# A third gate/up pair by quarter products, and a new order of casts, lesser parts and gates in two FFN openings

## The chip, the core and the metric

The kernel runs on one core of a Trainium2 chip. TensorE (PE) multiplies, VectorE (DVE) and ScalarE (ACT) do the elementwise work, GpSimd (POOL) issues some DMAs, and SyncE (SP) issues most of the others. Each engine works through its own queue in order; semaphores tie the queues together. The metric is the time of one execution in microseconds.

## The reference

The reference is one residual block over 512 tokens of width 1024:

```
h = h + 0.5 * swiglu_1(rmsnorm(h))                 # D_FF = 2816
z = rmsnorm(h) @ W_in ; conv module and gated linear attention
h = h + concat([y_conv, y_gla]) @ W_out
h = h + 0.5 * swiglu_2(rmsnorm(h))
h = h + sigmoid(rmsnorm(h) @ W_g) * (p @ W_p)
out = rmsnorm(h)
swiglu(x) = (silu(x @ W_gate) * (x @ W_up)) @ W_out
```

All of it is float32. The kernel holds every operand of a product as a high part (H, `wh`: the value rounded to the product's format) and a lesser part (L, `wl`: what is left of it), and does three products for each: high by high, high by lesser, lesser by high.

## The kernel before

**Pairs.** Each FFN layer takes the 2816 columns of gate and up in 11 pairs: a pair is 256 gate columns with the 256 up columns that belong to them. Its four weight tiles are `a11`, `a12` (gate, upper and lower half of the 1024 rows) and `a21`, `a22` (up). Each is fetched by one 512 KB DMA on SP into a ring of six buffers (`wr`), cast to `wh` on ACT, and its lesser part `wl` is a subtraction on DVE (`low`). `added` is another way to a lesser part: ACT writes the negated rounded value into `wl`, and a DMA on POOL's queue adds the unrounded `wr` to it.

**Two forms.** A plain pair is eight units h0 to h7, each of 12 products of 512 columns. A quarter pair works on sums and differences of the quarters of the weights and of the activations, as in Strassen's method in Winograd's form, and needs seven units of 24 products of 256 columns instead of what would be eight: m1, m2, m6, m7, m5, m4, m3. Its weights are a11, a12, s2, s3, s1, a22, s4, where s1 = a21 + a22, s2 = s1 - a11 and so on (DVE, tiles `sm` and `wr`); its activations are parts of the normalised input (`hg`) and four sums t1 to t4 of its quarters (DVE differences in tiles `xg`, then a cast `t2H` on ACT and a lesser part `t2L` on DVE, and likewise for the others). m1, m6, m5 and m3 add to one PSUM bank, and what the bank holds in between is needed too: ACT copies it out after m1 (`sq`), after m6 (`u`) and after m5 (`sq` again), and the next unit on that bank waits for the copy. After m2 the gate's first half is ready: two DVE operations and a silu on ACT (`gate0`, tiles `g` and `s`). After m5, m4 and m3 come the up products (`u`), the second half of the gate, the products `m`, and `act_parts`: two casts (`actH`) on ACT and two lesser parts (`actL`) on DVE for the output products.

**Order.** `drive` walks a list of units. Every unit has jobs with a distance: fetch, sum, cast and lesser part of a weight are put into the queues so many units ahead (`AHEAD` = 4 for a lesser part, 5 for m5's). What a unit leaves over (gates, act parts) is put in around the next unit. Output pieces of 24 products of 512 columns (`second`) follow a group of pairs and are strewn among the later units. Hooks at named units put other work in, such as the sums of the activations.

**The two layers.** In the first layer pair 0 is done while the input arrives, pairs 1 and 2 are plain (`plain` = (1, 2)), and pairs 3 to 10 are done by quarters; the sums t1 to t4 are spread over the units of pairs 1 to 3. In the second layer pair 0 is plain and done ahead of `ffn`; pairs 1 to 10 go by quarters. In that layer the first pair's `gate0` is held back to the end of its m5.

Of the kernel before, what the change touches and what calls it, by code (L numbers as in the profile page):

```python
# [62 lines left out]
def block_kernel(ctx: ExitStack, tc: tile.TileContext, a: dict, out: bass.AP):  # L63
    nc = tc.nc
    pe, dve, act, pool = (Ordered(tc, e) for e in (nc.tensor, nc.vector, nc.scalar, nc.gpsimd))
# [117 lines left out]
    def high(r3):  # L183

        nk, nc_ = r3.shape[1], r3.shape[2]
        hi = wp.tile([P, 1024], F32R, tag="wh", bufs=6, name=nm("wh"))
        lo = wp.tile([P, 1024], F32R, tag="wl", bufs=6, name=nm("wl"))
        h3 = hi[:, :nk * nc_].rearrange("p (k c) -> p k c", k=nk)
        l3 = lo[:, :nk * nc_].rearrange("p (k c) -> p k c", k=nk)
        act.copy(h3, r3)  # L190
        return h3, l3, r3

    def low(w, engine=dve):
        h3, l3, r3 = w
        engine.tensor_tensor(out=l3, in0=r3, in1=h3.bitcast(F32), op=ALU.subtract)
        return h3, l3
# [191 lines left out]
    class Left:  # L388


        def __init__(self, w, f):
            self.w, self.f, self.done = w, f, {}

        def fetch(self, *names):
            for name in names:
# [10 lines left out]
        def part(self, name, engine=None):  # L406

            if name not in self.done:
                self.done[name] = low(high(getattr(self, name)), engine or dve)
            return self.done[name]  # L410

        def add_part(self, *names):

# [23 lines left out]
    ffn1_in = a["ffn1_w_in"][0]  # L437
# [89 lines left out]
    mid = []  # L527
# [73 lines left out]
        for f in left:  # L601
            f()

    def ffn(w_in, w_out, x, gname, given, first, rsb, hooks, plain):


        norm = Norm()
# [1 line left out]
        got = {}  # L609
        npair = DFF // (2 * P)  # L610
        start = 1 + len(plain)
        held = []
        end = npair - 1
        pairs = {i: given.get(i) or Left(w_in, 2 * i) for i in range(npair)}

# [19 lines left out]
        def scaled(ps, name):  # L635
            o = tmp(name)
            dve.tensor_tensor(out=o, in0=ps, in1=got['rsb'], op=ALU.mult)
            return o

        def gated_block(p, s, u, i):  # L640
            if not hasattr(p, "m"):
                p.m = tmp("m", 2 * SEQ, bufs=1).rearrange("p (f c) -> p f c", f=2)
            dve.tensor_tensor(out=p.m[:, i], in0=u, in1=s, op=ALU.mult)
# [21 lines left out]
        def m2(p):  # L665
            p.y = bank()
            mul(p.y, p.part("a12"), x.op["b21"], True, True)

            def gate0():
                p.s0 = silu(plus(p.y, p.a, 0, "g1"))  # L670

            if p is pairs[start] and not plain:
                held.append(gate0)
                return []
            return [gate0]

# [8 lines left out]
        def m5(p):  # L685
            mul(p.x, p.part("s1"), x.op["t1"], False, False)
            p.u = plus(p.w, snap(p.x, "sq", bufs=3), 1, "u1")
            for f in held:
                f()
            held.clear()  # L690

        def m4(p):
            mul(p.w, p.part("a22"), x.op["t4"], False, True)
# [2 lines left out]
        def m3(p):  # L696
            mul(p.x, p.part("s4"), x.op["b22"], False, True)
            s = silu(times_row(p.x, 1, "g1"))
            return [lambda: gated(p, s, p.u, 1), lambda: act_parts(p)]

        def plain_unit(j):

            up, i, k = j // 4, j // 2 % 2, j % 2
            def run(p):
                if not j:
                    p.g, p.s = {}, {}
                if not k:
                    p.x = bank()
                ps = p.x
                wh, wl = p.part(f"a{1 + up}{1 + k}")  # L710
                cs = slice(i * P, (i + 1) * P)
                for c in range(4):
                    mm3(ps, wh[:, c, cs], wl[:, c, cs], *x.rows[4 * k + c], k == c == 0, k == 1 and c == 3)
                if not k:
                    return []
                if not up:
                    def gate():
                        p.s[i] = silu(scaled(ps, "g1"))
                    return [gate]
                return [lambda: gated_block(p, p.s[i], scaled(ps, "u1"), i),  # L720
                        lambda: act_parts(p) if i else None]
            return run

        USES = {"m1": ("a11", m1), "m2": ("a12", m2), "m6": ("s2", m6), "m7": ("s3", m7), "m5": ("s1", m5),
# [2 lines left out]
        def unit(kind, i):  # L727
            p = pairs[i]

            def go(run):  # L730
                left = run(p)
                hooks.get((kind, i), lambda *_: None)()
                return left

            if kind[0] == "h":
                j = int(kind[1])
                part, run = (f"a{1 + j // 4}{1 + j % 2}", plain_unit(j)) if j % 4 < 2 else (None, plain_unit(j))
                if part:
                    return [(AHEAD, lambda: p.part(part)), (9, lambda: p.fetch(part))], lambda: go(run)
            else:  # L740
                part, run = USES[kind]
            before = [(AHEAD + (kind == 'm5'), lambda: p.part(part))] if part else []
            if kind in ("m1", "m2"):
                before.append((7, lambda: p.fetch(part)))
            elif kind == "m6":
                before += [(9, lambda: p.fetch("a21", "a22")), (6, p.s12)]
            elif kind in ("m7", "m3"):
                before.append((6, p.s3_ if kind == "m7" else p.s4_))

            return before, lambda: go(run)  # L750

        def second(cut):
# [117 lines left out]
    def sums_hooks(x, names, at):  # L870

        h = {}
        for name, key in zip(names, at):
            h[key] = lambda *_, name=name: x.split(name)
        return h

    hooks = sums_hooks(xb, ("t2", "t3", "t1", "t4"), (("h5", 1), ("h7", 1), ("h3", 2), ("m1", 3)))
    hooks.update({("h%d" % (i + 1), 1): f for i, f in enumerate(steps[2:])})
    hooks.update({("m5", 3): lambda *_: made[0](), ("m5", 4): lambda *_: constants(),
                  ("m4", 10): lambda *_: w_ahead.append(ahead(w_in, D_CONV, 2 * P)),  # L880
                  ("last", 4): lambda *_: w_ahead.append(ahead(w_in, 0, 2 * P))})
    hg, norm = ffn(ffn1_in, a["ffn1_w_out"][0], xb, "mix_norm", {0: Left(ffn1_in, 0), 1: w1},
                   (ps0[:2], ps0[2:]), lambda: spread(mid[0]), hooks, (1, 2))
    pool.on = False
    cw, gwu, mean, mask, nbias = made

# [633 lines left out]
    def todo(*fs):  # L1520
# [5 lines left out]
                  ("rest", 2): todo((q_high, b21, q21, 0), (first_sum, 0), (third_sum, 0)),  # L1526
                  ("rest", 4): todo((q_high, b21, q21, 1), (first_sum, 1), (third_sum, 1)),
                  ("rest", 6): todo((final_in,), (row_sums, 0))})
    hg, norm = ffn(ffn2_in, a["ffn2_w_out"][0], xb, "ple_norm", wf, ((g0, u0), (g1_, u1_)), mid[1], hooks, ())

# [269 lines left out]
```

## Time and profile before

| | us |
|---|---|
| median of three runs | 949.35 (947.44 to 949.62) |
| the profiled execution | 948.38 |
| its span, first to last instruction | 946.7 |
| PE, DVE, ACT, POOL busy | 935.0, 755.6, 477.0, 57.2 |
| granted TensorE clock, mean | 0.996 |

A row of a timeline has start, duration, engine, line, operation, output and inputs, size and count; in square brackets stands how long the engine was idle before it and who ended that. All instructions go through one recording helper, line 46, so tiles tell them apart, not lines. Products are pipelined, so the duration of one is longer than the step from one to the next. A row of a window has its limits, the busy time with the number of instructions, the granted clock, the DMA share and GB/s. A row of PE's waits has what waited, for whom, the total, the number of times and the longest.

### The profile page before, as it was taken

To read this page: it belongs to the slowest core of one execution; us is meant where nothing else is said; L and a number is where in the kernel's file an instruction comes from. 1 tells how busy PE (TensorE), PEld (TensorE's weight loads), DVE (VectorE), ACT (ScalarE), POOL (GpSimd) and SP (SyncE) were. 2 spreads that over 40 slices of the span, in tenths; PEclk is the share of its full clock that TensorE was granted. 3 is DMA by queue.
4 is the path that set the end of the run, shared out by engine and by line. 5 is a ranking of instruction groups with operands and counts; after the bars stand their busy time and mean duration, and the time that the engine had idled before them with its cause. 6 is when DMAs were issued, how large, how long until landed. Compare 5 with 4: busy or idle time off the path is not lost.

```text
span 946.7 us, 14553 instructions
## 1 busy us (share of the span) xinstructions
PE 935.0 (99%) x5842; PEld 831.1 (88%) x5842; DVE 755.6 (80%) x1030; ACT 477.0 (50%) x720; POOL 57.2 (6%) x72
## 2 busy tenths in 40 slices
PE   9999999999999999999999999999999999999996
PEld 7888999999999988788877889899999999998885
DVE  5876887887788566999986788887878787866896
ACT  5652544434433574463564874444434433445882
POOL 0000200000000110001030020000000000000121
PEclk9999999999999999999999999999999999999998
DMA  7532323342323593346552572332243224347463
GB/s 229 180 114 72 106 69 117 105 131 80 103 90 111 140 257 83 81 102 167 134 126 77 154 163 82 112 114 88 90 134 112 67 91 133 96 147 225 89 113 110
DMA packets 107831, 113.43 MB, mean 120 GB/s; under 512 B 5155, under 2 KB 96469, under 8 KB 107764
## 3 DMA queue, kind: packets, MB, share of 16 engines
q1 hardware_dynamic: 101732, 94.67, 32.3%
q0 software_dynamic: 6016, 17.83, 10.4%
q8 instruction: 46, 0.75, 0.3%
q14 instruction: 21, 0.17, 0.1%
q10 hardware_dynamic: 16, 0.00, 0.0%
HBM read 93.61 MB, written 2.10 MB: 101 GB/s over the span
## 4 chain that ended last, share of the span: by engine, by line
PE 96%; DVE 2%; ACT 1%; issue 1%; POOLq 0%; POOL 0%; DVEq 0%; ACTq 0%
PE ps L46 94%; PE ax L46 2%; DVE wl L46 1%; DVE g L46 0%; ACT wh L46 0%; DVE u L46 0%; DVE wr L46 0%; ACT s L46 0%; DVE y L46 0%; DVE sm L46 0%; DVE actL L46 0%; DVE hgL L46 0%; ACT wl L46 0%; POOLq L1798 0%; ACT ycH L46 0%
## 5 line engine op out<-in xcount | busy, mean ns | idle before, releaser
L46 PE MATMUL ps<-hgH,wh 128*128 128x256 f32 (+1 forms) x768 | 235.9, 312 | 0.0
L46 PE MATMUL ps<-hgL,wh 128*128 128x256 f32 (+1 forms) x768 | 234.2, 310 | 0.0
L46 PE MATMUL ps<-hgH,wl 128*128 128x256 f32 (+1 forms) x768 | 234.0, 310 | 0.0
L46 DVE TENSOR_TENSOR wl<-wr,wh 128x1024 fp32r<-128x1024 f32 (+2 forms) x162 | 189.6, 1181 | 48.1 <-ACT wh L46 48.0
L46 ACT CAST wh<-wr 128x1024 fp32r<-128x1024 f32 (+2 forms) x177 | 177.8, 1019 | 39.8 <-PE ps L46 19.8
L46 PEld LDWEIGHTS ps<-hgH,wh 128*128 128x128 f32 x768 | 146.9, 192 | 9.9 <-issue 1.1
L46 PEld LDWEIGHTS ps<-hgH,wl 128*128 128x128 f32 x768 | 146.7, 191 | 7.8
L46 PEld LDWEIGHTS ps<-hgL,wh 128*128 128x128 f32 x768 | 146.3, 191 | 8.0 <-issue 0.2
L46 PE MATMUL ps<-actH,wh 128*128 128x512 f32 x352 | 137.4, 390 | 0.0
L46 PE MATMUL ps<-actL,wh 128*128 128x512 f32 x352 | 137.3, 390 | 0.0
L46 PE MATMUL ps<-actH,wl 128*128 128x512 f32 x352 | 136.9, 389 | 0.0
L46 ACT ACTIVATE s<-g 128x512 f32<-128x512 f32 x48 | 30.4, 633 | 190.2 <-DVE g L46 190.2
L46 DVE SCALAR_TENSOR_TENSOR cv<-glu,cw,cv 128x502 f32<-128x502 f32 (+24 forms) x120 | 81.0, 731 | 0.6
L46 PEld LDWEIGHTS ps<-actH,wl 128*128 128x128 f32 x352 | 66.1, 188 | 14.0
L46 PEld LDWEIGHTS ps<-actH,wh 128*128 128x128 f32 x352 | 66.2, 188 | 13.0
L46 PEld LDWEIGHTS ps<-actL,wh 128*128 128x128 f32 x352 | 66.2, 188 | 12.4
L46 DVE SCALAR_TENSOR_TENSOR h<-ps,h 128x512 f32<-128x512 f32 x80 | 53.9, 686 | 21.3 <-PE ps L46 21.2
L46 ACT COPY sq<-ps 128x512 f32<-128x512 f32 x40 | 23.3, 585 | 68.4 <-PE ps L46 68.3
L46 DVE TENSOR_TENSOR wl<-sm,wh 128x1024 fp32r<-128x1024 f32 x40 | 48.7, 1221 | 5.1 <-ACT wh L46 4.9
L46 ACT CAST wh<-sm 128x1024 fp32r<-128x1024 f32 x40 | 41.7, 1043 | 7.0 <-DVE sm L46 4.2
L46 ACT CAST actH<-m 128x512 fp32r<-128x512 f32 x44 | 25.4, 618 | 38.5 <-DVE m L46 38.4
L46 PE MATMUL ps<-t1H,wh 128*128 128x256 f32 x144 | 40.9, 284 | 1.0 <-ACT u L46 1.0
(267 smaller groups left out, 1744.2 us busy)
## 6 DMA issues: line engine op xcount, KB each, us to landing
wr<-in_ffn_w_in SPq DMA_DIRECT2D x84, 512.0 KB
wr<-in_ffn_w_out SPq DMA_DIRECT2D x32, 512.0 KB
wr<-in_w_in SPq DMA_DIRECT2D x20, 512.0 KB
wl<-wr POOLq DMA_DIRECT2D x16, 512.0 KB, 5.5
wr<-in_ffn_w_out SPq DMA_DIRECT2D x16, 384.0 KB
wr<-in_w_out SPq DMA_DIRECT2D x8, 512.0 KB
wq<-in_ple_w_gate SPq DMA_DIRECT2D x8, 512.0 KB
wl<-wq POOLq DMA_DIRECT2D x8, 512.0 KB, 5.3
```

The source lines that it names most:

```text
L46: inst = call(*args, **kwargs)
```

## The change

In the first layer only pair 1 stays plain; pair 2 goes by quarters, so the sums t2, t3 and t1 are made during pair 1 and t4 at pair 2's m1. Some weights get their cast one unit ahead of the lesser part (`cast`, the table CASTS), some lesser parts stand three units ahead instead of four or five (FAR), and two of them, pair 1's a21 and pair 2's a12, are made by `added` (ADDS). In the second layer four distances change, s2 of pair 2 is cast early, and s1 and s3 of pair 2 are cast ahead of pair 1's `gate0`. In both layers `act_parts` of every pair but the last is put behind the next pair's m6 instead of around the unit after m3, and pair 1's last gate product and act parts in the first layer go behind m6 of pair 2.

```diff
+        def cast(self, *names):
+            for name in names:
+                self.cut[name] = high(getattr(self, name))
...
-    def ffn(w_in, w_out, x, gname, given, first, rsb, hooks, plain):
+    def ffn(w_in, w_out, x, gname, given, first, rsb, hooks, plain, far={}, casts={}, adds=()):
...
-            if p is pairs[start] and not plain:
-                held.append(gate0)
+            if p is pairs[start]:
+                after["m5", start] = [gate0] if plain else [lambda: pairs[start + 1].cast("s1", "s3"), gate0]
                 return []
...
-            return [lambda: gated(p, s, p.u, 1), lambda: act_parts(p)]
+            if p is pairs[end]:
+                return [lambda: gated(p, s, p.u, 1), lambda: act_parts(p)]
+            after["m6", p.f // 2 + 1] = [lambda: act_parts(p)]
+            return [lambda: gated(p, s, p.u, 1)]
...
-                return [lambda: gated_block(p, p.s[i], scaled(ps, "u1"), i),
+                last = [lambda: gated_block(p, p.s[i], scaled(ps, "u1"), i),
                         lambda: act_parts(p) if i else None]
+                if i and p is pairs[start - 1]:
+                    after["m6", start] = last
+                    return []
+                return last
...
                 left = run(p)
+                for f in after.pop((kind, i), ()):
+                    f()
                 hooks.get((kind, i), lambda *_: None)()
...
-            before = [(AHEAD + (kind == 'm5'), lambda: p.part(part))] if part else []
...
+            if (kind, i) in casts:
+                before.append((casts[kind, i], lambda: p.cast(part)))
+            if part:
+                make = p.add_part if (kind, i) in adds else p.part
+                before.append((far.get((kind, i), AHEAD + (kind == "m5")), lambda: make(part)))
...
-    hooks = sums_hooks(xb, ("t2", "t3", "t1", "t4"), (("h5", 1), ("h7", 1), ("h3", 2), ("m1", 3)))
-    hooks.update({("h%d" % (i + 1), 1): f for i, f in enumerate(steps[2:])})
+    hooks = sums_hooks(xb, ("t2", "t3", "t1", "t4"), (("h4", 1), ("h5", 1), ("h7", 1), ("m1", 2)))
+    w2 = Left(ffn1_in, 4)
+    hooks.update({("h0", 1): steps[2], ("h1", 1): steps[3],
+                  ("h4", 1): lambda *_: [steps[4](), xb.split("t2")],
+                  ("h5", 1): lambda *_: [xb.split("t3"), w2.s12()]})
...
-                   (ps0[:2], ps0[2:]), lambda: spread(mid[0]), hooks, (1, 2))
+    FAR = {("h5", 1): 3, ("m1", 2): 3}
+    CASTS = {("h5", 1): 4, ("m1", 2): 4}
+    ADDS = {("h4", 1), ("m2", 2)}
...
+                   (ps0[:2], ps0[2:]), lambda: spread(mid[0]), hooks, (1,), FAR, CASTS, ADDS)
...
-    hg, norm = ffn(ffn2_in, a["ffn2_w_out"][0], xb, "ple_norm", wf, ((g0, u0), (g1_, u1_)), mid[1], hooks, ())
+    hg, norm = ffn(ffn2_in, a["ffn2_w_out"][0], xb, "ple_norm", wf, ((g0, u0), (g1_, u1_)), mid[1], hooks, (), {("m5", 1): 4, ("m6", 2): 3, ("m1", 3): 3, ("m2", 3): 3}, {("m6", 2): 4})
```

The first place that the prediction speaks of is DVE's queue in the first layer, behind the act parts of pair 0 (tiles end in a buffer number). Before, from a22's lesser part of pair 1 to that of pair 2's a12:

```order
L46 TENSOR_TENSOR wl_483<-wr_429,wh_482 128x1024
L46 TENSOR_TENSOR xg_416<-xg_422,xg_416 128x512
L46 TENSOR_TENSOR xg_422<-xg_422,xg_413 128x512
L46 TENSOR_TENSOR xg_419<-xg_419,xg_422 128x512
L46 TENSOR_TENSOR g_111_507<-ps_439,bc_457 128x512
L46 TENSOR_TENSOR xg_498<-xg_501,xg_498 128x512
L46 TENSOR_TENSOR xg_501<-xg_527,xg_501 128x512
L46 TENSOR_TENSOR xg_527<-xg_527,xg_498 128x512
L46 TENSOR_TENSOR xg_524<-xg_524,xg_527 128x512
L46 TENSOR_TENSOR wl_549<-wr_431,wh_548 128x1024
L46 TENSOR_TENSOR g_119_552<-ps_511,bc_457 128x512
L46 TENSOR_TENSOR wl_572<-wr_433,wh_571 128x1024
```

Now, behind three differences (`xg`), from the fourth to the lesser part of pair 2's a11, which m1 of pair 2 uses:

```order
L46 TENSOR_TENSOR xg_479<-xg_482,xg_479 128x512
L46 TENSOR_TENSOR wl_491<-wr_429,wh_490 128x1024
L46 TENSOR_TENSOR g_115_519<-ps_436,bc_454 128x512
L46 TENSOR_TENSOR g_121_553<-ps_523,bc_454 128x512
L46 TENSOR_TENSOR xg_482<-xg_508,xg_482 128x512
L46 TENSOR_TENSOR xg_508<-xg_508,xg_479 128x512
L46 TENSOR_TENSOR xg_505<-xg_505,xg_508 128x512
L46 TENSOR_TENSOR t2L_574<-xg_422,t2H_573 128x512
L46 TENSOR_TENSOR t2L_578<-xg_508,t2H_577 128x512
L46 TENSOR_TENSOR sm_581<-wr_512,wr_514 128x1024
L46 TENSOR_TENSOR sm_582<-sm_581,wr_488 128x1024
L46 TENSOR_TENSOR wl_551<-wr_488,wh_550 128x1024
```

The lesser part of a22 (`wr_429`) stands behind four differences now, and t2's lesser parts and pair 2's sums s1 and s2 (`sm`) stand ahead of the first lesser part of pair 2.

The second place is ACT's queue in the second layer at the copy `sq` after pair 1's m1. Before:

```order
L46 ACTIVATE s_5496<-g_960_5494 128x512
L46 CAST wh_5505<-sm_5376 128x1024
L46 COPY sq_5534<-ps_5509 128x512
L46 CAST actH_5536<-m_5492 128x512
L46 CAST actH_5540<-m_5492 128x512
```

Now:

```order
L46 ACTIVATE s_5596<-g_970_5594 128x512
L46 COPY sq_5630<-ps_5605 128x512
L46 CAST actH_5632<-m_5592 128x512
L46 CAST actH_5636<-m_5592 128x512
L46 CAST wh_5640<-sm_5476 128x1024
```

The cast of s1 (`wh<-sm`) has moved from ahead of the copy to behind the act casts of pair 0.

The third place is ACT's queue a little later, from the copy `sq` after pair 1's m5 to the copy `u` after pair 2's m6. Before:

```order
L46 COPY sq_5695<-ps_5509 128x512
L46 ACTIVATE s_5703<-g_987_5700 128x512
L46 CAST wh_5707<-sm_5605 128x1024
L46 CAST wh_5711<-wr_5501 128x1024
L46 ACTIVATE s_5745<-g_996_5742 128x512
L46 CAST wh_5776<-wr_5665 128x1024
L46 ACTIVATE s_5806<-g_1002_5804 128x512
L46 CAST wh_5812<-wr_5705 128x1024
L46 COPY u_1008_5841<-ps_5578 128x512
```

Now:

```order
L46 COPY sq_5794<-ps_5605 128x512
L46 CAST wh_5799<-sm_5705 128x1024
L46 CAST wh_5802<-wr_5601 128x1024
L46 ACTIVATE s_5808<-g_1001_5805 128x512
L46 ACTIVATE s_5845<-g_1006_5842 128x512
L46 ACTIVATE s_5902<-g_1010_5900 128x512
L46 CAST wh_5908<-wr_5765 128x1024
L46 COPY u_1016_5937<-ps_5678 128x512
```

The casts of s1 and s3 of pair 2 stand ahead of pair 1's silu, the cast of pair 3's a11 (`wr_5765`) stands behind the last silu, and that of pair 3's a12 has left the stretch.

More of the change, by code (lines that the diff above doesn't have):

```diff
@@ L391, in __init__ @@
         def __init__(self, w, f):
-            self.w, self.f, self.done = w, f, {}
+            self.w, self.f, self.done, self.cut = w, f, {}, {}
         def fetch(self, *names):
@@ L408, in part @@
             if name not in self.done:
-                self.done[name] = low(high(getattr(self, name)), engine or dve)
+                self.done[name] = low(self.cut.pop(name, None) or high(getattr(self, name)), engine or dve)
             return self.done[name]
+        def cast(self, *names):
+            for name in names:
+                self.cut[name] = high(getattr(self, name))
         def add_part(self, *names):
@@ L611, in ffn @@
         start = 1 + len(plain)
-        held = []
+        after = {}
         end = npair - 1
@@ L687, in m5 @@
             p.u = plus(p.w, snap(p.x, "sq", bufs=3), 1, "u1")
-            for f in held:
-                f()
-            held.clear()
         def m4(p):
@@ L737, in unit @@
                 part, run = (f"a{1 + j // 4}{1 + j % 2}", plain_unit(j)) if j % 4 < 2 else (None, plain_unit(j))
-                if part:
-                    return [(AHEAD, lambda: p.part(part)), (9, lambda: p.fetch(part))], lambda: go(run)
+                before = [(9, lambda: p.fetch(part))] if part else []
             else:
                 part, run = USES[kind]
-            before = [(AHEAD + (kind == 'm5'), lambda: p.part(part))] if part else []
+                before = []
             if kind in ("m1", "m2"):
@@ L881, in block_kernel @@
                   ("last", 4): lambda *_: w_ahead.append(ahead(w_in, 0, 2 * P))})
-    hg, norm = ffn(ffn1_in, a["ffn1_w_out"][0], xb, "mix_norm", {0: Left(ffn1_in, 0), 1: w1},
-                   (ps0[:2], ps0[2:]), lambda: spread(mid[0]), hooks, (1, 2))
+    FAR = {("h5", 1): 3, ("m1", 2): 3}
+    CASTS = {("h5", 1): 4, ("m1", 2): 4}
+    ADDS = {("h4", 1), ("m2", 2)}
+    hg, norm = ffn(ffn1_in, a["ffn1_w_out"][0], xb, "mix_norm", {0: Left(ffn1_in, 0), 1: w1, 2: w2},
+                   (ps0[:2], ps0[2:]), lambda: spread(mid[0]), hooks, (1,), FAR, CASTS, ADDS)
     pool.on = False
```

## The prediction

> **What bounds the kernel now.** I read the page first, then TensorE's waits, then windows over single kinds of products, and last the timelines of the two openings, where an FFN layer starts on its quarter products.
>
> ```profile
> span 946.7 us, 14553 instructions
> PE 935.0 (99%) x5842; PEld 831.1 (88%) x5842; DVE 755.6 (80%) x1030; ACT 477.0 (50%) x720; POOL 57.2 (6%) x72
> ...
> PE ps L46 <- ACT u L46: 1.0, 1, 1.0
> ...
> PE ps L46 <- ACT sq L46: 0.2, 1, 0.2
> ```
>
> TensorE (PE) is busy 99% of the span, so time can be won in two ways only: fewer or shorter products, or fewer waits of PE. Two of its waits name ScalarE (ACT) tiles that this change touches, and both lie in the second layer's opening. How long a product takes is read from start to start:
>
> ```profile
> 38.20:59.96 21.76, 21.76 (x98) 1.00 0.29 91
> 62.76:68.20 5.44, 5.44 (x26) 1.00 0.36 104
> 601.83:607.30 5.47, 5.47 (x27) 1.00 0.32 95
> 621.40:632.90 11.50, 11.50 (x98) 1.00 0.30 93
> ...
> 35.45 0.48 PE L46 MATMUL ps<-hgH,wh 128*128 128x512 f32 x1
> ```
>
> Each window runs from the first start of its products to the start of the next one; the counts take in neighbours that overlap the edges. The first holds eight plain units, 96 products of 512 columns: 21.76/96 = 0.2267 us. The last holds four quarter units, 96 products of 256 columns: 11.50/96 = 0.120 us. So 512 columns cost 0.2267, not 2 x 0.120 = 0.240. The two in the middle are output pieces of 24 products: 5.44 us among products of their own width, 5.47 among quarter units.
>
> **Fewer products (first layer).** Pair 2 leaves the plain form, 96 x 0.2267 = 21.76 us, for seven quarter units, 168 x 0.120 = 20.16 us: **-1.60 us**. Four output pieces now stand among quarter units: 4 x 0.03 = **+0.11 us**, rounded down from 0.12. Everything on PE after them comes earlier, so this is on the path, provided that the operands are ready. The Trainium skill ("TensorE: Matmul & The Clock Gate", Back-to-back issue gap) gives a warm gap of N/2.4 ns plus 2.5 ns, 215.8 and 109.2 ns here; the sum would be 20.72 - 18.34 = 2.38 us saved instead of 1.60. The rows above are some 11 ns longer for either width, and the trace decides.
>
> **The cover in that opening.** The rows on VectorE (DVE) and ACT that price it:
>
> ```profile
> 33.99 1.05 ACT L46 CAST wh<-wr 128x1024 fp32r<-128x1024 f32 x1
> 35.73 0.59 ACT L46 COPY bc<-ax 128x512 f32<-128x512 f32 x1 [0.69 <-PE ax L46]
> ...
> 546.08 1.06 ACT L46 ACTIVATE wl<-wr 128x1024 fp32r<-128x1024 f32 x1
> 547.04 1.03 ACT L46 CAST wh<-wr 128x1024 fp32r<-128x1024 f32 x1
> ...
> 42.62 1.23 DVE L46 TENSOR_TENSOR wl<-wr,wh 128x1024 fp32r<-128x1024 f32 x1 [0.26 <-ACT wh L46]
> 43.76 2.14 DVE L46 TENSOR_TENSOR xg<-xg,xg 128x512 f32<-128x512 f32 x3
> 45.82 0.68 DVE L46 TENSOR_TENSOR g<-ps,bc 128x512 f32<-128x512 f32 x1
> 46.42 0.68 DVE L46 TENSOR_TENSOR xg<-xg,xg 128x512 f32<-128x512 f32 x1
> ...
> 88.05 1.22 DVE L46 TENSOR_TENSOR sm<-wr,wr 128x1024 f32<-128x1024 f32 x1
> 89.30 1.23 DVE L46 TENSOR_TENSOR sm<-sm,wr 128x1024 f32<-128x1024 f32 x1
> ...
> 53.15 0.63 ACT L46 ACTIVATE s<-g 128x512 f32<-128x512 f32 x1 [3.07 <-DVE g L46]
> 53.68 1.03 ACT L46 CAST wh<-wr 128x1024 fp32r<-128x1024 f32 x1
> 54.62 1.14 ACT L46 CAST t2H<-xg 128x512 fp32r<-128x512 f32 x2
> ...
> 553.77 1.05 ACT L46 ACTIVATE wl<-wr 128x1024 fp32r<-128x1024 f32 x1
> ...
> 555.12 0.86 POOL L46 DMA_DIRECT2D wl<-wr  x1 [4.92 <-ACT wl L46]
> ...
> L46 POOL DMA_DIRECT2D wl<-wr x16: 859/862/919, 376.4 to 565.2; - x16
> ...
> DMA to landing us min/median/max: 4.5/5.5/9.9
> ```
>
> From start to start a lesser part (wl) takes DVE 1.14, three chained differences 2.06, a lone 512-wide operation 0.60, two chained sums 1.25 + 1.14.
>
> PE runs h1 from 35.45; with 12 x 0.2267 = 2.72 per plain unit and 2.88 per quarter unit, h4 starts at 43.6, h5 at 46.3, m1 of pair 2 at 54.5, m2 at 57.4. A lesser part is first used in a unit's third product, whose weights load one product earlier: one product after the unit's start.
>
> Pair 1's a21 now gets its lesser part by a negated copy on ACT (0.96, from 546.08 to 547.04) and an accumulating DMA from POOL. The copy follows the cast of 33.99 and pushes bc from 35.73 to 35.89; the gates behind it go 0.16 later, and DVE, which is free at 42.36 in this trace (42.62 less the 0.26 of waiting), is free at 42.5. Then, by the new order: three differences to 44.56, a fourth to 45.16, a22's lesser part done 1.22 later at 46.38, used by h5 at 46.56. Two gate products to 47.5, three differences to 49.56, t2's lesser parts (the first waits for its cast until 49.65) to 50.85, s1 and s2 to 53.24, a11's lesser part of pair 2 done at 54.46, used by m1 at 54.6. Both are in time by 0.1 to 0.2 us, which is less than I can be sure of.
>
> Pair 2's a12 goes the way of POOL: ACT's silu at 46.99 (behind its gate product), cast 47.52, silu 48.46, t2's casts 48.99 and 49.51, a12's cast 50.03, negation 50.97 to 52.03, DMA issued at about 52.3 (0.3 behind, as 555.12 is behind 553.77 + 1.05). With the quickest landing, 4.5, it is there at 56.8, with the median of 5.5 at 57.8; m2 uses it at 57.5. So PE waits 0 to 0.3 us there. I take 0.15 us for all three places, between 0 and 1 us (my timeline may be off by so much). Queued behind: the refill of a21's buffer on SP waits for the first DMA's landing near 41, and the rest of SP's queue with it; it brings pair 3's a11, which ACT casts near 53. Later deadlines have room: s3 is done near 64 for m7 at 66.0, s4 and the up product before m4 (77) for 80.1.
>
> **The second layer's two waits.**
>
> ```profile
> 568.38 0.28 PE L46 MATMUL ps<-hgH,wl 128*128 128x256 f32 x1
> 568.86 0.39 PE L46 MATMUL ps<-t2H,wh 128*128 128x256 f32 x1 [0.20 <-ACT sq L46]
> ...
> 591.87 0.28 PE L46 MATMUL ps<-t3H,wl 128*128 128x256 f32 x1
> 593.10 0.39 PE L46 MATMUL ps<-t1H,wh 128*128 128x256 f32 x1 [0.95 <-ACT u L46]
> ...
> 567.29 1.04 ACT L46 CAST wh<-sm 128x1024 fp32r<-128x1024 f32 x1
> 568.23 0.58 ACT L46 COPY sq<-ps 128x512 f32<-128x512 f32 x1
> ...
> 591.00 0.63 ACT L46 ACTIVATE s<-g 128x512 f32<-128x512 f32 x1 [2.28 <-DVE g L46]
> 591.53 1.03 ACT L46 CAST wh<-wr 128x1024 fp32r<-128x1024 f32 x1
> 592.47 0.58 ACT L46 COPY u<-ps 128x512 f32<-128x512 f32 x1
> ...
> 578.99 0.68 DVE L46 TENSOR_TENSOR u<-ps,sq 128x512 f32<-128x512 f32 x1
> 583.42 1.23 DVE L46 TENSOR_TENSOR wl<-sm,wh 128x1024 fp32r<-128x1024 f32 x1 [1.70 <-ACT wh L46]
> 590.22 0.68 DVE L46 TENSOR_TENSOR g<-ps,bc 128x512 f32<-128x512 f32 x1
> ```
>
> PE's normal step is 0.12, so the first gap, 568.38 to 568.86, holds 0.36 of waiting: m6 cannot add to the bank before ACT's copy sq is out, and that copy stands behind s1's cast. The new order puts the cast behind the copy and the act casts; sq is done at 567.29 + 0.58 = 567.87, before 568.50: **-0.36 us**. s1 is then cast by about 569.9 and its lesser part is done by 571.2; m5 needs it at 574.3, so the cover is three us.
>
> The second gap, 591.87 to 593.10, holds 1.11: m5 of pair 2 needs ACT's copy u out of the bank, and ACT was late because it waits 2.28 for the gate product g of 590.22, a row of DVE. DVE itself had idled 1.70 at 583.42 for a cast. In the new order s1 and s3 of pair 2 are cast before pair 1's silu, so that idle goes; a11's lesser part of pair 3 moves behind g, and s2's comes ahead of it in exchange (1.14 each). The chain from the row u<-ps,sq to g takes 590.22 - 578.99 = 11.23 now. It starts at 578.3 instead (PE is 0.36 earlier, and s2's lesser part no longer stands ahead of it), so g starts at 578.3 + 11.23 - 1.70 = 587.8. Silu, cast and copy follow: the silu from 588.4, the cast from about 589.0, the copy from 589.9 to 590.5. m5 would start at 591.6, so **-1.11 us** goes whole. Late next is a12's lesser part of pair 3: DVE does a11's part behind its cast from 590.05 (1.14), the product m (0.69), waits for the first act cast (0.67), two act parts (1.25), s4 (1.14), the output piece's part (1.14) and then this one (1.22), to 597.3, and m2 wants it at 591.6 + 2 x 2.88 + 0.12 = 597.4. Bounds 0 to 0.6; I take **+0.15 us**.
>
> The act casts of every later pair move behind the copy u, in both layers. They are used four units later, so I cost them at nothing; the cover is over 11 us of quarter units. The other instructions that move keep their counts; the two lesser parts that left DVE cost ACT 2 x 0.96 and POOL two issues of 0.86, beside PE.
>
> **The sum.** The profiled run took 948.38 us (span 946.7 and 1.7 around it). 948.38 - 1.60 + 0.11 + 0.15 - 0.36 - 1.11 + 0.15 = 945.7. That profile lies 0.97 under the median of 949.35; the other runs go from 947.44 to 949.62, so I say **945.8 us**, 0.37% under the median. About 0.3% (2.85 us) is what a measurement of this kernel tells from no change: faster means under 946.5, slower over 952.2.
>
> **Rivals.**
>
> *One gain is lost, 946.9 us.* If DVE's queue in the first opening is 1.5 us later than I have it, m1 of pair 2 waits that long and 948.38 - 0.36 - 1.11 is left; if the second opening's wait only moves to m2 of pair 3, it is 948.38 - 1.60 + 0.11. For it speak margins of 0.1 us; against it that all steps are measured in the same opening. Chance 0.20, within 0.3%.
>
> *POOL's DMA comes late, 950 to 953 us.* At the longest landing seen, 9.9, pair 2's a12 is there at 62.2 and m2 waits 4.7: 948.38 - 1.49 - 1.47 + 4.7 = 950.1. Over a landing of 5.2 it starts to cost, at 7.9 it eats all. And where PE stands still, the granted clock falls:
>
> ```profile
> 938.00:947.00 9.00, 0.03 (x1) 0.61 0.31 117
> ```
>
> Were the clock to stay at that 0.61 for as long as the wait lasted, the products of 4.7 us would take 4.7 x (1/0.61 - 1) = 3.0 us more, an estimate from that row: 953.1. Against it: 9.9 is the longest, nearly twice the median, and few fetches fall into this stretch. Chance 0.16, half of it over 952.2. The Trainium skill ("SBUF — State Buffer", SBUF: two separate sides) says that a DMA issued from POOL waits for its descriptors while VectorE runs an operation in a two-port mode, which would make such lateness usual. By that rule the issue would be long in some of the 16 rows; they lie between 859 and 919 ns with VectorE at work, so the trace does not bear it out.
>
> *Products as short as the formula, 944.9 us.* If quarter units of pair 2 gained 0.8 more, because a product had a smaller fixed cost in this place than in the windows: 945.7 - 0.8. No row supports it. Chance 0.05; the skill's gap, above, is this case.
>
> My forecast, 944.9 to 946.5, has 0.55; 0.04 is left for what I have not seen, on the slow side. Faster 0.60, same 0.20 + 0.08 = 0.28, slower 0.08 + 0.04 = 0.12. The range leaves out the late DMA and the unseen (0.20): from 944.2 (the formula's case less half the runs' scatter) to 948.6 (one gain lost and a slow run).
>
> **What would show it.** PE's waits for ACT sq and ACT u gone near 568 and 593; 72 more instructions on PE; h5, m1 and m2 of the first layer without a gap over 0.3 us. Wrong would be a PE wait for POOL's wl before m2, for DVE's wl at h5 or m1, or for DVE's wl at m2 of pair 3 in the second layer.

## The result, and the profile after

| | before | changed |
|---|---|---|
| median, us | 949.49 (947.44 to 949.74, six runs) | 944.67 (944.09 to 946.14, six runs) |
| ratio, with its 95% interval | | 0.9956 (0.9943 to 0.9969) |
| the profiled execution (its span) | 948.38 (946.7) | 944.09 (942.4) |

The changed kernel is 0.44% faster by these medians. The page of the changed kernel, and the list of what TensorE (PE) waited for:

```profile
PE 931.9 (99%) x5914; PEld 832.6 (88%) x5914; DVE 762.2 (81%) x1038; ACT 481.9 (51%) x728; POOL 57.0 (6%) x74
...
PE ax L46 <- POOL ident masks.py:199: 1.6, 1, 1.6
PE ps L46 <- ACT ycH L46: 0.2, 1, 0.2
```

PE has 72 more instructions and is busy 3.1 us less. Both waits on ScalarE (ACT) tiles that the prediction quoted are gone, and no wait has taken their place.

To see where the time went, I cut each span at three products that every version has: the first one of h1 in the first layer, the first one behind the four transposes that spread the second layer's row norms, and the first one of the second layer's first output piece. First the kernel before, then the changed one; a row has its limits and its length:

```profile
35.45:549.56 514.11, 513.88 (x3157) 1.00 0.42 114
549.56:601.83 52.27, 51.12 (x385) 1.00 0.50 122
```

```profile
34.43:547.03 512.60, 512.37 (x3229) 1.00 0.44 117
547.03:597.65 50.62, 50.62 (x384) 1.00 0.52 128
```

The first stretch holds pair 2 and the first opening: 1.51 us less. The second holds the second opening: 1.65 less. Together 3.16. The profiled executions differ by 4.29; of the rest, 1.02 lies ahead of h1 (35.45 against 34.43), where both kernels run the same code on PE, and 0.1 behind the second stretch. The runs below show what that is.

In the first opening of the changed kernel, rows on VectorE (DVE), POOL and PE (PEld is the load of a product's weights), and last the landing of the accumulating DMA issued at 51.37:

```profile
35.51 0.69 DVE L46 TENSOR_TENSOR g<-ps,bc 128x512 f32<-128x512 f32 x1 [1.71 <-ACT bc L46]
...
44.10 1.22 DVE L46 TENSOR_TENSOR wl<-wr,wh 128x1024 fp32r<-128x1024 f32 x1
...
52.27 1.22 DVE L46 TENSOR_TENSOR wl<-wr,wh 128x1024 fp32r<-128x1024 f32 x1
...
51.37 0.86 POOL L46 DMA_DIRECT2D wl<-wr  x1 [14.98 <-DVE sm L46]
...
45.88 0.39 PE L46 MATMUL ps<-hgH,wl 128*128 128x512 f32 x1
...
53.58 0.28 PE L46 MATMUL ps<-hgH,wh 128*128 128x256 f32 x1
...
53.70 0.19 PEld L46 LDWEIGHTS ps<-hgH,wl 128*128 128x128 f32 x1
...
56.70 0.28 PE L46 MATMUL ps<-hgH,wl 128*128 128x256 f32 x1
...
DMA to landing us min/median/max: 4.6/4.6/4.6
```

DVE idles 1.71 for bc ahead of the first gate product. A lesser part is the weight of a unit's third product, and that weight is loaded while the second product runs: m1 starts at 53.58, and its load of a lesser part (`wl`) at 53.70. So the margins count to the load. a22's lesser part is done at 45.32, and h5 loads it at 45.65, one product ahead of the row of 45.88: 0.33 to spare. a11's lesser part of pair 2 is done at 53.49, 0.21 ahead of m1's load. The DMA has landed at 51.37 + 4.6 = 56.0, and m2's load runs at 56.58, one product ahead of 56.70: 0.6 to spare. In the second opening, on PE, ACT and DVE:

```profile
565.98 0.28 PE L46 MATMUL ps<-t2H,wh 128*128 128x256 f32 x1
...
589.01 0.28 PE L46 MATMUL ps<-t1H,wh 128*128 128x256 f32 x1
...
564.76 0.57 ACT L46 COPY sq<-ps 128x512 f32<-128x512 f32 x1
...
587.41 0.57 ACT L46 COPY u<-ps 128x512 f32<-128x512 f32 x1
...
592.40 3.49 DVE L46 TENSOR_TENSOR wl<-wr,wh 128x1024 fp32r<-128x1024 f32 x3
```

The copy sq is out at 565.33, 0.65 before m6; the copy u at 587.98, 1.03 before m5 of pair 2. The three lesser parts in a row on DVE have a12's of pair 3 as the second: it ends at 592.40 + 1.14 + 1.22 = 594.76, and m2's load of it runs one product behind the unit's start, at 589.01 + 2 x 2.88 + 0.12 = 594.89. That is 0.13 to spare, the least of these margins.

### The profile page after: what moved, and what is told of

The parts are those of the page before. It is cut to its first block, busy times and chain, and to the rows that moved or that the text cites. A ratio compares the mean times of both kernels' runs of the same rounds, so it can differ in the third digit from the quotient of the medians.

```text
span 942.4 us, 14718 instructions
## 1 busy us (share of the span) xinstructions
PE 931.9 (99%) x5914; PEld 832.6 (88%) x5914; DVE 762.2 (81%) x1038; ACT 481.9 (51%) x728; POOL 57.0 (6%) x74
## 4 chain that ended last, share of the span: by engine, by line
PE 99%; DVE 0%; ACT 0%; POOLq 0%; issue 0%; POOL 0%
PE ps L46 97%; PE ax L46 1%; DVE y L46 0%; POOLq L1818 0%; ACT ycH L46 0%; DVE yc L46 0%; ACT hgH L46 0%; DVE rs L46 0%; ACT s L46 0%; DVE u L46 0%; DVE g L46 0%; DVE s L46 0%; POOL ident masks.py:199 0%; DVE ms L46 0%; POOL mean L46 0%
## 5 line engine op out<-in xcount | busy, mean ns | idle before, releaser
L46 PE MATMUL ps<-hgH,wh 128*128 128x256 f32 (+1 forms) x768 | 231.6, 307 | 0.1
L46 PE MATMUL ps<-hgL,wh 128*128 128x256 f32 (+1 forms) x768 | 230.8, 306 | 0.0
L46 PE MATMUL ps<-hgH,wl 128*128 128x256 f32 (+1 forms) x768 | 230.5, 305 | 0.0
L46 DVE TENSOR_TENSOR wl<-sm,wh 128x1024 fp32r<-128x1024 f32 x42 | 51.1, 1222 | 8.5 <-ACT wh L46 8.5
L46 DVE TENSOR_TENSOR actL<-m,actH 128x512 fp32r<-128x512 f32 x44 | 28.6, 689 | 33.4 <-ACT actH L46 33.2
L46 ACT COPY u<-ps 128x512 f32<-128x512 f32 x19 | 11.1, 587 | 75.0 <-PE ps L46 75.0
L46 ACT CAST wh<-sm 128x1024 fp32r<-128x1024 f32 x42 | 43.8, 1043 | 3.6 <-DVE sm L46 2.0
```

The source lines that it names most:

```text
L46: inst = call(*args, **kwargs)
```

## The experiments

The stretches are those above. Runs of the kernel before beside the experiments had their lowest at 947.39 to 947.49 each time, and medians of 947.74 (23 runs; e1, e2, e4, e7), 948.12 (12; e5, e6, e8, e9) and 947.99 (19; e3, e10, e11). Ratios are to those.

| | median, us | ratio (95%) | first stretch | second stretch | h1 starts |
|---|---|---|---|---|---|
| before | | | 514.11 | 52.27 | 35.45 |
| changed | | | 512.60 | 50.62 | 34.43 |
| e9, changed again | 944.83 | 0.9959 (0.9946 to 0.9973) | 512.59 | 50.62 | 36.58 |
| e1, second layer alone | 946.63 | 0.9983 (0.9974 to 0.9992) | 514.18 | 50.62 | 36.57 |
| e2, first layer alone | 946.59 | 0.9982 (0.9973 to 0.9991) | 512.62 | 52.27 | 34.63 |
| e3, no tables | 945.41 | 0.9976 (0.9966 to 0.9985) | 512.86 | 50.62 | 35.31 |
| e4, no adds | 945.14 | 0.9969 (0.9958 to 0.9980) | 513.38 | 50.63 | 36.39 |
| e10, one add | 944.75 | 0.9968 (0.9957 to 0.9978) | 512.59 | 50.62 | 34.57 |
| e5, s1's cast ahead | 944.85 | 0.9965 (0.9952 to 0.9979) | 512.62 | 51.07 | 34.75 |
| e6, casts behind the silu | 946.10 | 0.9978 (0.9967 to 0.9988) | 512.60 | 52.20 | 35.18 |
| e11, no later parts | 944.86 | 0.9967 (0.9954 to 0.9980) | 512.62 | 50.88 | 35.49 |

The stretches of versions that are alike repeat within 0.07 us. The start of h1 goes over 2.15 us between versions with the same code on PE ahead of it. So differences of some tenths are read from the stretches, one profile for each version; the medians of 4 to 11 runs don't tell them. e5 is 0.45 longer than the changed kernel in its second stretch, and its median is 944.85 beside e9's 944.83.

### The two halves alone (e1, e2)

e1, in the first layer (with the sums' hooks as before, and the rules for `gate0` and `act_parts` confined to the second):

```diff
-                   (ps0[:2], ps0[2:]), lambda: spread(mid[0]), hooks, (1,), FAR, CASTS, ADDS)
+                   (ps0[:2], ps0[2:]), lambda: spread(mid[0]), hooks, (1, 2))
```

> The first layer is as before (pairs 1 and 2 plain); the second layer has all of the change. Theory A (the ledger): only the two ScalarE waits of the second opening go, 0.36 + 1.11 and about 0.09 of restart behind each, so 1.65 us under the kernel before, 947.8 against 949.5; TensorE's waits list neither ACT u nor ACT sq; m1 of pair 1 in the second layer starts as far behind h1 of the first layer as before. Theory B (the extra 1.0 us at the start of the changed kernel belongs to the change): the same here, since the first layer is as before, but h1 starts at 35.4 as before. By A the start of h1 lies anywhere between 34.4 and 35.4, whatever the kernel. Theory C (act casts behind the copy u cost something later): a gain under 1 us.

e2, in the second layer (with `act_parts` there in its old place):

```diff
-                after["m5", start] = [gate0] if plain else [lambda: pairs[start + 1].cast("s1", "s3"), gate0]
+                after["m5", start] = [gate0]
...
-    hg, norm = ffn(ffn2_in, ..., hooks, (), {("m5", 1): 4, ("m6", 2): 3, ("m1", 3): 3, ("m2", 3): 3}, {("m6", 2): 4})
+    hg, norm = ffn(ffn2_in, ..., hooks, ())
```

> The second layer is as before; the first layer has all of the change. Theory A: 96 x 0.2267 - 168 x 0.120 = 1.60 less, 0.11 given back by the output pieces, so 1.5 us under the kernel before, 948.0 against 949.5; the stretch from h1 of the first layer to m1 of pair 1 of the second is 1.5 shorter, and the waits for ACT sq (0.36 over the step) and ACT u (1.11) stand as before. Theory B (the early start belongs to the change, in the first layer): 2.5 under before, 947.0, with h1 at 34.4.

The second stretch of e1, then the first of e2:

```profile
550.75:601.37 50.62, 50.62 (x384) 1.00 0.52 128
```

```profile
34.63:547.25 512.62, 512.38 (x3230) 1.00 0.43 117
```

Each half takes its own part of the gain, 1.65 and 1.49, and leaves the other stretch as before (514.18, 52.27). The halves add up and don't touch each other. On the medians they are 1.11 and 1.15, and on the lowest runs 1.57 and 1.74; these hold the start of every run as well. Theory B falls: h1 starts at 36.57 in e1 and 34.63 in e2, but in e9, the changed kernel itself, at 36.58. Theory C falls as well: from the second stretch to the end e1 takes 344.7 us, and the kernel before 344.9.

### The changed kernel again (e9), and when TensorE comes to speed

> The changed kernel itself, once more beside the kernel before on another day's chip. Theory A: what the change does is 3.16 us of TensorE's time between the first product behind the first opening's norm (h1) and the end; the rest of the first measurement's 4.8 came from when TensorE went to full speed in the first ten microseconds of each execution, which is the same code in both. Then the difference of the medians lies between 2 and 5, the lowest runs of both differ by 3.2 to 3.4, and h1 starts anywhere from 34.4 to 36.6. Theory B (all of it belongs to the change): again 4.5 to 5 us, h1 at 34.4.

The ratio is 0.9959 against 0.9956. The medians differ by 3.29 and the lowest runs by 3.11, a little under the 3.2 to 3.4 that I expected; theory B's 4.5 to 5 didn't come again. This time the profiled execution took 946.26 us instead of 944.09, 2.17 more, and its h1 starts 2.15 later, while both stretches are the same to 0.01. So nearly the whole difference of these two executions lies ahead of h1, in the first eleven microseconds. First the kernel before (the last row is a window: limits, length, busy time with the number of products, granted clock), then the changed kernel, then e9:

```profile
6.22 2.05 PE L46 MATMUL ps<-hgH,wh 128*128 128x512 f32 x4
8.07 1.15 PE L46 MATMUL ps<-hgH,wl 128*128 128x512 f32 x4
...
6.00:8.00 2.00, 2.00 (x6) 1.00 1.00 329
```

```profile
6.16 1.20 PE L46 MATMUL ps<-hgH,wh 128*128 128x512 f32 x4
7.19 1.07 PE L46 MATMUL ps<-hgH,wl 128*128 128x512 f32 x4
...
6.00:8.00 2.00, 1.95 (x9) 1.00 0.82 273
```

```profile
6.37 2.05 PE L46 MATMUL ps<-hgH,wh 128*128 128x512 f32 x4
8.21 1.91 PE L46 MATMUL ps<-hgH,wl 128*128 128x512 f32 x4
```

Four products of 512 columns take 2.05 or 1.91 at half speed, 1.20 or 1.07 at full speed. Full speed came near 6.2 in the changed kernel, near 8.2 in the kernel before, and after 9.9 in e9. The column of the granted clock says 1.00 in all of them; only the steps tell.

Two experiments tried to bring that moment forward. e7 gives PE something to do before the identity matrix is there, and e8 the same with one product and eight transposes (its second cut shows the lines that differ):

```diff
+    early = cp.tile([P, P], F32, name="early")
+    dve.memset(early, 1.0)
+    idle = aux()
+    for _ in range(3):
+        pe.matmul(idle[:, 0:P], early, early, start=True, stop=True)
     warm_up(10)
```

> As the changed kernel, with three 128-column products on a tile of ones that VectorE sets, ahead of the ten transposes at the start: TensorE begins near 0.6 us instead of 1.61. The first eight 512-column products ran at 0.42 us each in the profile of before and at 0.24 in that of the changed kernel, with the same code there. Theory A1 (TensorE goes to full speed a fixed time after its first work): all products behind the transposes at full speed, h1 at 34.4 or earlier, 0.3 to 1 us under the changed kernel on the median and less scatter. Theory A2 (the moment comes from a clock that runs on its own): no difference on the median, h1 still between 34.4 and 35.4.

```diff
+    pe.matmul(idle[:, 0:P], early, early, start=True, stop=True)
-    warm_up(10)
+    warm_up(8)
```

> As the changed kernel, with one 128-column float32 product on ones that VectorE sets, and eight transposes behind it instead of ten: TensorE starts at 1.12 instead of 1.61 and is ready for the input at 4.07 as before (the three products of the run before this one made the first input transposes 1.1 late). Theory A (TensorE goes to full speed at the end of the first window of a free-running clock, some 3.4 us long, in which it was busy throughout): the moment comes 0.5 earlier in some executions and a whole window earlier in others; on the mean 0.2 to 0.5 us under the changed kernel on the same chip, h1 at 34.4 in more of the runs, lowest run as the changed kernel's lowest. Rival (the moment doesn't depend on when TensorE starts): the same mean and scatter.

PE began at 1.12 in both. (The text on e7 has the first eight products of 512 columns at half speed in the kernel before; by the rows above it was the first four.) In e7 PE was at full speed by 5.34, but the extra products made the transposes of the input late, so that the first product of 512 columns started at 6.77; the median was 945.17, a ratio of 0.9970. In e8 that product started at 6.29 and full speed came near 8.6; the median was 945.29 (944.11 to 946.49), on a chip where the changed kernel had 944.83. From 1.12 the moment came 4 us after PE's first work once and 7.5 once; from 1.61 between 3.5 (e2) and more than 8.3 (e9). So it doesn't come a fixed time after PE's first work (A1), and an early start won nothing that five or six runs show. Nor is an early moment all gain: in e2 and e5, at full speed by 5.2, PE then waited 0.73 and 0.76 for the first `wh` from DVE, and h1 started at 34.63 and 34.75, not ahead of the changed kernel's 34.43. What sets the moment, none of these runs settles.

### The first layer's tables (e4, e10, e3)

e4, and e10, which keeps one of the two:

```diff
-    ADDS = {("h4", 1), ("m2", 2)}
+    ADDS = ()
```

> As the changed kernel, but pair 1's a21 and pair 2's a12 get their lesser parts on VectorE instead of by the accumulating DMA. Theory A (margins of 0.1 to 0.2 us in the first opening are real): a21's part costs nothing, since VectorE idled 1.71 us ahead of the first gate product; a12's part puts 1.14 ahead of a11's, which then ends at 54.6 in the changed kernel's time where m1 of pair 2 needs it at 53.8: TensorE waits 0.8 there, and some 0.2 more for s2's part at m6. 1.0 us over the changed kernel, 945.7. Rival (the margins are wider than the timeline says, or the two DMAs buy nothing): 944.7, no wait.

```diff
-    ADDS = {("h4", 1), ("m2", 2)}
+    ADDS = {("m2", 2)}
```

> As the changed kernel, but pair 1's a21 gets its lesser part on VectorE, and only pair 2's a12 by the accumulating DMA. Theory A: VectorE idled 1.71 us ahead of the first gate product, the part fills 1.14 of that, and ScalarE loses a negated copy of 0.96 in front of bc; behind the plain units' gate products, which wait for TensorE, everything stands as in the changed kernel. No difference: 944.8, no wait of TensorE in the opening. Rival (the part is late for the chain of gate products): up to 0.8 us over, with a wait at h5 or m1.

PE at m1 of pair 2 and the first stretch in e4, then DVE and the first stretch in e10:

```profile
55.66 0.28 PE L46 MATMUL ps<-hgL,wh 128*128 128x256 f32 x1
56.44 0.19 PEld L46 LDWEIGHTS ps<-hgH,wl 128*128 128x128 f32 x1 [0.70 <-DVE wl L46]
56.44 0.38 PE L46 MATMUL ps<-hgH,wl 128*128 128x256 f32 x1 [0.50 <-DVE wl L46]
56.67 0.28 PE L46 MATMUL ps<-hgH,wh 128*128 128x256 f32 x1
...
36.39:549.77 513.38, 512.64 (x3229) 1.00 0.42 114
```

```profile
34.22 1.23 DVE L46 TENSOR_TENSOR wl<-wr,wh 128x1024 fp32r<-128x1024 f32 x1 [0.27 <-ACT wh L46]
...
34.57:547.16 512.59, 512.36 (x3229) 1.00 0.43 116
```

In e4 the step from 55.66 to 56.44 is 0.78 where 0.12 is normal, a wait of 0.66, and the next step is 0.23, 0.10 too long: 0.77, the 0.78 of the stretch. It is the load that waits, from 55.66, where it would have run with the second product, to 56.44: 0.78 again. The margin at m1 is real and smaller than the 1.14 of one lesser part. The wait that I also expected at m6 didn't come; I had put m6 right behind m2, and m1 of pair 3 stands between them, so s2's part has 2.9 us more. e10 shows that all of the 0.78 hangs on pair 2's a12. Pair 1's a21 can be made on DVE in the time in which it waits for bc anyway; its accumulating DMA buys nothing.

e3 empties all three tables:

```diff
-    FAR = {("h5", 1): 3, ("m1", 2): 3}
-    CASTS = {("h5", 1): 4, ("m1", 2): 4}
-    ADDS = {("h4", 1), ("m2", 2)}
+    FAR = {}
+    CASTS = {}
+    ADDS = ()
```

> As the changed kernel, but in the first layer without both accumulating DMAs, without the early casts and with all distances as in the code before. Theory A: a11's lesser part of pair 2 comes at 47 and a12's in place of it at 54.6, in time for m1 (53.8) and m2 (56.7); VectorE has 1.14 more to do by m6, whose lesser part ends at 60.5 in the changed kernel's time where 59.6 is needed: 0.9 to 1.0 us over the changed kernel, 945.8, TensorE's wait at m6 and none at h5 or m1. Rival (the order of the table is what makes pair 2 fit at all): several waits, 2 us or more over.

DVE ahead of a11's lesser part of pair 2, the same part of pair 3 with its load and product in m1, and the first stretch:

```profile
48.31 1.23 DVE L46 TENSOR_TENSOR wl<-wr,wh 128x1024 fp32r<-128x1024 f32 x1 [1.70 <-ACT wh L46]
...
59.18 1.22 DVE L46 TENSOR_TENSOR wl<-wr,wh 128x1024 fp32r<-128x1024 f32 x1
...
60.45 0.19 PEld L46 LDWEIGHTS ps<-hgH,wl 128*128 128x128 f32 x1
60.46 0.39 PE L46 MATMUL ps<-hgH,wl 128*128 128x256 f32 x1
...
35.31:548.17 512.86, 512.63 (x3230) 1.00 0.43 115
```

DVE idles 1.70 for a cast that stands behind a silu on ACT, which the early cast in the changed kernel avoids. Yet the price is 0.26, in m1 of pair 3 and at m7, not the 0.9 to 1.0 at m6 that I expected by the same slip. At m1 the part is done at 59.18 + 1.22 = 60.40; the load would have run at 60.33 and runs at 60.45, the product comes on time at 60.46, and the next step is 0.10 too long all the same. Of the 1.51 us of the first layer, 1.25 come without the tables, and the tables add the rest. The old distances with the quarter form (e3) even do better than the new distances without the DMAs (e4): what one table does depends on the others.

### The second layer's order (e5, e6, e11)

e5 and the expectation:

```diff
-{("m5", 1): 4, ("m6", 2): 3, ("m1", 3): 3, ("m2", 3): 3}
+{("m6", 2): 3, ("m1", 3): 3, ("m2", 3): 3}
```

> As the changed kernel, but m5 of pair 1 in the second layer has its lesser part five units ahead again, so s1's cast stands ahead of the copy sq. Theory A: the silu there starts at 564.23 in the changed kernel's time; the cast takes 564.76 to 565.70, the copy ends at 566.28, and m6, which would start at 565.98, waits 0.30 and starts its row 0.10 slower: 0.4 us over the changed kernel from one opening to the other, 945.1. The wait for ACT u stays away. Rival (that wait went because pair 0's products came earlier, not by the cast's place): no wait, 944.7.

```profile
566.19 0.28 PE L46 MATMUL ps<-hgH,wl 128*128 128x256 f32 x1
566.67 0.39 PE L46 MATMUL ps<-t2H,wh 128*128 128x256 f32 x1 [0.20 <-ACT sq L46]
566.89 0.28 PE L46 MATMUL ps<-t2L,wh 128*128 128x256 f32 x1
...
565.10 1.04 ACT L46 CAST wh<-sm 128x1024 fp32r<-128x1024 f32 x1
566.04 0.58 ACT L46 COPY sq<-ps 128x512 f32<-128x512 f32 x1
```

The old wait is back, as in the profile of before: 0.36 over the step, and 0.10 in the step behind it. The second stretch is 0.45 longer. One number in the table of distances is worth 0.45 of the second layer's gain, with the rest of the order in place.

e6, which keeps all distances:

```diff
-                after["m5", start] = [gate0] if plain else [lambda: pairs[start + 1].cast("s1", "s3"), gate0]
+                after["m5", start] = [gate0]
```

> As the changed kernel, but s1 and s3 of pair 2 in the second layer are cast behind pair 1's silu again. Theory A: VectorE idles 1.7 us ahead of their lesser parts, so the gate product at 585.16 in the changed kernel's time comes at 586.9, silu, cast and copy u follow to 589.7, and m5, which would start at 589.01, waits 0.7 and 0.1 more for the slower row: 0.8 us over the changed kernel, 945.5; the list of TensorE's waits has ACT u with 0.7. So of the 1.2 us of that wait 0.8 hang on these two casts and 0.4 on the lesser parts' other places. Rival (the distances of the lesser parts took the wait away, not the casts): no wait, 944.7.

DVE, three places on PE, and the second stretch:

```profile
580.81 1.23 DVE L46 TENSOR_TENSOR wl<-sm,wh 128x1024 fp32r<-128x1024 f32 x1 [1.69 <-ACT wh L46]
...
584.36 0.39 PE L46 MATMUL ps<-t2H,wl 128*128 128x256 f32 x1
...
590.48 0.39 PE L46 MATMUL ps<-t1H,wh 128*128 128x256 f32 x1 [0.34 <-ACT u L46]
...
596.46 0.28 PE L46 MATMUL ps<-hgL,wh 128*128 128x256 f32 x1
597.24 0.39 PE L46 MATMUL ps<-hgH,wl 128*128 128x256 f32 x1 [0.50 <-DVE wl L46]
...
547.78:599.98 52.20, 51.36 (x385) 1.00 0.50 123
```

I expected 0.8 and measured 1.58, nearly all that the second layer had won. The idle time of 1.69 is as expected, but it is paid in three places, not one: 0.12 at m6 of pair 2 (s2's part), 0.50 at m5 (copy u), 0.66 at m2 of pair 3 (a12's part, 596.46 to 597.24), and 0.10 behind each. The last of them is the place where the prediction expected the next lateness.

e11 keeps the casts and gives up the other distances:

```diff
-{("m5", 1): 4, ("m6", 2): 3, ("m1", 3): 3, ("m2", 3): 3}, {("m6", 2): 4})
+{("m5", 1): 4})
```

> As the changed kernel, but without the second layer's shorter distances for s2 of pair 2 and a11 and a12 of pair 3, and without the early cast of s2; the casts of s1 and s3 stay ahead of pair 1's silu. Theory A (those casts are what took the wait for ACT u away): a11's lesser part stands 1.14 ahead of the gate product again, which comes at 586.3 in the changed kernel's time, and with silu, one cast and the copy u that ends at 589.1, where m5 would start at 589.01: 0.1 to 0.2 us over the changed kernel, 945.0. Rival (the distances share the gain evenly with the casts): 0.8 us over, 945.6, with the wait for ACT u at 0.7.

```profile
590.09 0.28 PE L46 MATMUL ps<-t3H,wl 128*128 128x256 f32 x1
590.25 0.39 PE L46 MATMUL ps<-t1H,wh 128*128 128x256 f32 x1
590.48 0.28 PE L46 MATMUL ps<-t1L,wh 128*128 128x256 f32 x1
...
548.11:598.99 50.88, 50.88 (x384) 1.00 0.51 125
```

0.26 us more, where I expected 0.1 to 0.2, in two waits of 0.03 to 0.04 (one is at 590.25, for the copy u, as expected), each with a slow step of 0.10 behind it. So the two casts and m5's distance keep 1.39 of the 1.65, and all distances without the casts (e6) are worth almost nothing: 52.20 against 52.27. What each piece is worth depends on the others; their losses taken out one by one (0.45, 1.58, 0.26) sum to more than the gain.

## Why the prediction came out right

The forecast was 945.8 and faster, with 944.2 to 948.6 as its range; the median was 944.67. By its steps:

- **Fewer products** (-1.60, +0.11 for output pieces): right. Forecast -1.49, measured -1.51 in the changed kernel and -1.49 in e2. The steps of 0.2267 and 0.120 held for pair 2. The gap by the formula in the Trainium skill ("TensorE: Matmul & The Clock Gate", Back-to-back issue gap), which the page calls that of an isolated product, would have made this 0.8 larger; the trace disagrees, and that rival falls.
- **The first opening's three places** (+0.15): nothing was paid. The DMA for a12 landed 4.6 after its issue, the short end of the 4.5 to 9.9 that I had, and 4.6 or 4.7 in the eight other versions that have it; at the median of 5.5 it would have been 0.3 late for m2's load. h5 had 0.33 and m1 0.21 to spare where I had seen 0.1 to 0.2. That the part is needed one product ahead of its use was right (e3, e4), and so was that these margins are narrow: 1.14 more on DVE ahead of a11's part costs 0.78 (e4).
- **The copy sq** (-0.36): right in place and cause (e5), short by the slow step of 0.10 behind the wait.
- **The copy u** (-1.11): right, with the same 0.10 missing. The cause was as told, the casts ahead of the silu (e6 loses it, e11 nearly keeps it), and so was the chain: the gate product comes at 585.16 in the changed kernel, 3.85 ahead of m5 of pair 2, and I had it 3.8 ahead. That e6 pays in three places shows that "the idle goes" was worth more than this one wait.
- **Late next at m2 of pair 3** (+0.15): the place was right (e6), and so was the margin (0.1 forecast, 0.13 measured), but in the changed kernel nothing waits there.
- **The act casts behind u** (nothing): the stretches leave no room for a cost.

On the trace the terms sum to -2.66 and the stretches to -3.16. The step that was off in size is the pair of +0.15s, 0.30, which measured zero, and the slow steps behind the two waits, 0.2, which I hadn't priced though the rows at 568.86 and 593.10 show them as a duration of 0.39 instead of 0.28. From 948.38 the sum would then have been 945.2. The rest, 945.2 to 944.67, and the gap of the first measurement between 3.2 and 4.8, are well within what the start moves (2.15); for the profiled executions that is shown, for the runs without a profile it is argued. The median of the kernel before was 949.49 beside the first measurement and 947.74 to 948.12 in 54 later runs, so some 1.6 of the first measurement's 4.8 is the luck of that draw: the stretches give 3.2 and e9's medians 3.3. I had read the 0.97 between the profiled run and the median as scatter and not looked for its place.

Of the rivals, the late DMA didn't happen. Whether VectorE was ever in the two-port mode that the prediction set beside it, no row here says. "One gain is lost" didn't happen either, but both of its places wait as soon as one part of the order is taken out: 0.66 at m1 in e4, 0.66 at m2 of pair 3 in e6.

## What to carry to other kernels

When an engine is 99% busy, cut its span at products that both versions have and compare the stretches: here they repeat within 0.07 us where the total goes over 2 us by itself. A wait of TensorE is to be priced with the slow step behind it, so that even 0.03 us of waiting costs 0.13, and an operand has to be there one product early, when it is loaded. And a cast moved ahead of something that ACT must wait for can be worth more than the one wait that the list of waits shows, because everything queued on DVE behind the missing cast comes late too.

## What the runs showed of the hardware

- **The start.** PE ran at half speed (512 columns in 0.43 us) until a moment that lay before 5.1 us in e2 and after 9.9 in e9, in executions of the same code, which moved h1 between 34.43 and 36.58; the granted clock read 1.00 throughout. In e2 the transposes are at full speed early (four in 0.60; in the changed kernel and the kernel before the same four took 0.93 and 1.06):

```profile
5.06 0.60 PE L46 MATMUL ax<-ident 128*128 128x128 f32 x4
```

The Trainium skill ("TensorE: Matmul & The Clock Gate", What's actually happening) describes a free-running window of about 3.4 us in which PE must have been busy, and a moment that varies by about 0.5 us either way; it adds that the number of slow products differs from run to run. That the moment isn't tied to PE's first work agrees with e7 and e8; the spread here is near 5 us, ten times the half-microsecond and more than one window.

- **The step behind a wait.** After every wait of PE among the quarter units of the two openings the waiting 256-column product shows 0.38 to 0.39 instead of 0.28, and the next one starts 0.22 to 0.23 behind it instead of 0.12, however short the wait was (0.03 in e11, 0.66 in e4). In the rows of these waits the load of the weights starts together with its product (both at 56.44 in e4), where otherwise it runs one product ahead. In e3 the load alone was late and the step of 0.22 came without a wait of the product. So the load that nothing covers fits the 0.10; no run tests it further.
